# Expert slots of 32, 64 and 64 + 32 tokens in plain float32 in a two-block kernel, and a state-space product whose two column halves alternate

## Chip, cores and metric

One core of a Trainium2 chip. The metric is device time in microseconds of the whole program; lower is better.

## The reference

Two transformer-like blocks over 512 tokens of width 1024, batch 1, float32. The first block mixes tokens (an in-projection, two state-space scans with heads of 64, a Fourier branch, an output projection) and then runs a mixture of 32 experts; the second is attention beside a gated recurrence, with a dense feed-forward. The part at issue is mostly the mixture: each token goes to its four best experts, and an expert's work on the rows it got is

```python
gu = xe @ w_gate_up[e] + b_gate_up[e]                       # 1024 -> 2048
gate = jnp.minimum(gu[:, :D_FF], SWIGLU_LIMIT)
up = jnp.clip(gu[:, D_FF:], -SWIGLU_LIMIT, SWIGLU_LIMIT)
act = (up + 1.0) * gate * jax.nn.sigmoid(SWIGLU_ALPHA * gate)
return act @ w_down[e] + b_down[e]                          # 1024 -> 1024
```

weighted by the softmax of the four logits and added to the token. Each expert has 12 MB of float32 weights, 384 MB for all 32, and 512 x 4 = 2048 rows are shared out among them, 64 on average. The reference's own routing of its inputs gives experts 0 and 1 25 and 23 rows; the other thirty, sorted, get 16 to 30 (six of them), 34 to 63 (eight), 66 to 95 (twelve), 109, 128, 130 and 155.

## The kernel before, in words

**The mixture (`moe`, from L1169).** The experts are put into 32 slots: slots 0 and 1 are experts 0 and 1, the others are sorted by load on the chip (`router`, `slot` and `perm`). A slot has a fixed room: slots 0 to 15 (`HALF`) one block of 64 rows, 16 to 29 one of 128, 30 and 31 (`DOUBLE`) one of 128 and one of 64. What doesn't fit goes through a loop at the end (`For_i`), one block of 128 rows a pass. `ORDER` is the order in which the slots are worked on, one slot a turn.

A turn is `up` of its own slot and then `down` of the slot before. `up` walks through eight raw tiles of `w_gate_up` of 1 MB each (L61), `down` through four of `w_down` (L1348). All loads go out on SyncE's queue, in the order of their use, into a ring of 13 tiles (`W.rings`): a load is issued when the tile 13 loads earlier has been read for the last time. So the loads run at most 13 tiles, about one turn, ahead.

- A block of 128 rows works on weights split into a high part (ScalarE, L86) and a low part (VectorE, L87) in a format that TensorE takes at one row of the moving operand after the other; each product is three matmuls (`mm3`, L99 to L101): 12 matmuls of 512 columns per MB.
- A block of 64 rows takes the raw weights in plain float32 (`half_mm`, L1262): the rows are stationary, 64 columns of the array wide, and the two halves of the output columns go to the two halves of the array. The profile shows a float32 matmul as two instructions, so there are 8 per MB.

In a turn with two blocks, `up` and `down` go through both blocks for each tile of weights. Around this lie the gather of the rows (GpSimd, L1227), their transposes on TensorE (L1245, L1240 for halves), the bias matmuls (L1254), the activation (`swiglu`, L1267 to L1270), the scaling of the result (ScalarE L1331, GpSimd L1336) and the scatter that adds to the token's row (L1337). Two steps hooked into `up` make the tables of later blocks (`table`, L1075 to L1081; `slots`) and transpose the previous slot's activations; one hooked into `down` transposes the next slot's rows. For slot 0 the rows aren't gathered but picked out by matmuls in `router` (L975).

**The state-space part (`mixer`).** For each of 16 pairs of heads, `py` collects 16 products of float32 (two heads j, two directions d, four blocks b of 128 tokens; L669), each two instructions on 64 columns of the array: head 0 writes partitions 0 to 63, head 1 partitions 64 to 127. The loops run j, d, b from outside in. The masks `m` come by DMA (L619) in the order j, d.

Two places in the first half load `w_mod` and multiply it by one vector with 32 stationary columns, four such matmuls into the four quarters of the array (L266, L515).

Of the kernel before, what the change touches and what calls it, by code (L numbers as in the profile page):

```python
# [8 lines left out]
F32 = mybir.dt.float32  # L9
# [95 lines left out]
TILE_WAITS = ('moeio', 'moeio3', 'ps_g', 'ps_mt', 'ps_d', 'outr', 'outp', 'mx', 'biasp', 'rows', 'b2io', 'b2t', 'b2r', 'res2', 'moeT', 'wraw3', 'wraw4')  # L105


class Kernel:
# [91 lines left out]
    def mixer(self):  # L200
# [391 lines left out]
        for p in range(16):  # L592
# [22 lines left out]
            for j in range(2):  # L615
                for d in range(2):
# [269 lines left out]
    def router(self, mx, keep, xT, ahead, st, stp):  # L886
# [59 lines left out]
        def choose(b, x1, rs, fill=lambda: None):  # L946
# [23 lines left out]
            self.chosen = nc.vector.tensor_scalar(pick[:, b, :], iota[:, 0:64], r[:, 0:1], None, op0=ALU.is_equal).ins  # L970
# [18 lines left out]
        pick = xT[:, 0:256].rearrange("p (b l) -> p b l", l=64)  # L989
# [17 lines left out]
        xT4 = xT[:, 512:].rearrange("p (k t) -> p k t", k=4)  # L1007
        nc.scalar.copy(xT4[:, 0:2, :], pts[0][:, 0:2, :])
        nc.vector.tensor_copy(xT4[:, 2:4, :], pts[0][:, 2:4, :])
        ahead()  # L1010

        with self.behind((self.chosen,)):
            p0 = psl.tile([P, 1, 3], F32, tag='ptab', name='ptab0')
            self.table(rot, p0[:, 0, :], rm[:, :, 1:2], V[:, :, 1, 0:3], True, True)
            first = self.slots(keep, p0, 1, 'f', (0,))[0]
# [53 lines left out]
    def table(self, pool, out, place, v, first, half=False):  # L1069
# [3 lines left out]
        v4 = lambda x: x.rearrange("p b (h l) -> p b h l", h=2)  # L1073
        if half:
            nc.vector.tensor_tensor(v4(pe), self.rc[:, 0, None, None, 0:64].to_broadcast([P, NT, 2, 64]),  # L1075
                                    place[:, :, :, None].to_broadcast([P, NT, 2, 64]), op=ALU.is_equal)
# [16 lines left out]
    def overflow(self, tp, psl, selb, ubf, obf, keep):  # L1093
# [3 lines left out]
        nc, cf = self.nc, self.rc  # L1097
# [10 lines left out]
        val = tp.tile([P, 2, 16], BF16, name='val')  # L1108
        for i, c in enumerate((16, 40)):
            nc.vector.tensor_scalar(val[:, i, :], cf[:, 2, 24:40], pos, cf[:, 2, c:c + 1], op0=ALU.is_equal, op1=ALU.mult)  # L1110
        nc.tensor.matmul(pc[:, 8:40], obf, val.rearrange("p i q -> p (i q)"), start=True, stop=True,
                         skip_group_check=True)
        nc.tensor.matmul(pc[:, 40:41], obf, fl, start=True, stop=True, skip_group_check=True)
        self.ext = ext = keep.tile([P, 33], F32, name='ext')
        nc.vector.tensor_copy(ext, pc[:, 8:41])

        no = tp.tile([P, 16], F32, name='noblk')
        nc.vector.tensor_scalar(no, ext[:, 16:32], 0.0, 4096.0, op0=ALU.is_equal, op1=ALU.mult)
        nc.vector.tensor_add(ext[:, 16:32], ext[:, 16:32], no)
        self.exti = keep.tile([P, 33], I32, name='exti')  # L1120
# [23 lines left out]
    def slots(self, pool, tab, n, sfx, halves=()):  # L1144


        nc = self.nc
        t = pool.tile([P, n, tab.shape[2]], F32, name='slott' + sfx)
# [6 lines left out]
        for j in halves:  # L1155
            nc.vector.tensor_scalar(f[:, 0, j:j + 1], f[:, 0, j:j + 1], 2.0, self.rc[:, 2, 41:42], op0=ALU.mult, op1=ALU.add)
        nc.vector.tensor_copy(i, f[:, 0, :])
        if tab.shape[2] > 3:
# [5 lines left out]
    HALF = range(0, 16)  # L1164
    DOUBLE = (30, 31)
    ORDER = (0, 1, 16, 17, 2, 3, 18, 19, 4, 20, 5, 21, 6, 30, 7, 8, 22, 9, 23, 10, 24, 11, 31, 12, 13, 25, 26, 14, 27, 28,
             29, 15)

    def moe(self, mx):  # L1169
# [39 lines left out]
        halfrows = lambda t: t.rearrange("s (h c) -> (s h) c", h=2)  # L1209
# [7 lines left out]
        io3 = self.pool('moeio3', 4, None, st)  # L1217
# [7 lines left out]
        def gather(i, tok, half=False):  # L1225
            x = xgs[i % 2]
            nc.gpsimd.indirect_dma_start(out=x[:, :D // 2] if half else x, out_offset=None,  # L1227
                                         in_=halfrows(self.h2_d) if half else self.h2_d,
                                         in_offset=bass.IndirectOffsetOnAxis(ap=tok, axis=0),
                                         bounds_check=(2 * S if half else S) - 1, oob_is_err=False)  # L1230
            return x

        def transposed(half, src, scale):
# [3 lines left out]
            if half:  # L1237
                h = src[:, 512:].rearrange("p (k t) -> p k t", k=4)
                for k in range(4):
                    nc.tensor.transpose(pt[:, k, :], src[:, k * P:(k + 1) * P], self.ident)  # L1240
                nc.scalar.activation(h, pt[:, 0:4, :], AF.Copy, scale=scale)  # L1241
                return half, h
            h = Ts[next(turns) % 2]
            for k in range(KD):
                nc.tensor.transpose(pt[:, k, :], src[:, k * P:(k + 1) * P], self.ident)  # L1245
            split_scaled(nc, h, pt, scale)
            return half, h

        def bias(half, outs, selT, c):

            w = 64 if half else P
            for i, o in enumerate(outs):
                for q in range(P // w):
                    nc.tensor.matmul(o[w * q:w * q + w], selT.to_broadcast([96, w]),  # L1254
                                     bh[:, c + 512 * (i * (P // w) + q):][:, :512], start=True, stop=False,
                                     skip_group_check=half)
# [15 lines left out]
        def up(xTs, rows, selT, step=None):  # L1272

            acts, pgs = [], []
            for half, _ in xTs:
                acts.append((half, io3.tile([P, D], F32, tag='row', name='act')))
                if not half:
                    pgs.append([bank2(ps_g, 'pg', 'pg') for _ in range(2)])
                    for i in range(2):
                        bias(half, (pgs[-1][i][:, 0, :], pgs[-1][i][:, 1, :]), selT, D * i)  # L1280
                else:
                    pgs.append(bank2(ps_d, 'pd', 'pgh') if len(xTs) == 2 else bank2(ps_g, 'pg', 'pgh'))
                    bias(half, (pgs[-1][:, 0, :], pgs[-1][:, 1, :]), selT, 0)
            for k, raw in enumerate(rows):
                for (half, x), pg in zip(xTs, pgs):
                    for h in range(2):
                        if half:
# [707 lines left out]
```

## Time and profile before

| what | value |
|---|---|
| median of 3 runs (2915.26 to 2928.36) | 2924.7 us |
| the profiled execution's own time | 2918.13 us |
| its span, first to last instruction | 2916.3 us |
| mean granted TensorE clock | 0.984 of full speed |
| bytes moved by DMA | 644.40 MB |

PE is TensorE's matmuls, PEld its loads of the stationary operand, DVE VectorE, ACT ScalarE, POOL GpSimd, SP SyncE, whose instructions here only issue loads. In the rows, `out<-in` names the tiles, 128\*64 means 128 rows and 64 columns of the array, and x is a count. A matmul's duration holds its way through the array, so a string of matmuls is priced by the distance from one start to the next.

### The profile page before, as it was taken

To read this page: it belongs to the slowest core of one execution; us is meant where nothing else is said; L and a number is where in the kernel's file an instruction comes from. 1 tells how busy PE (TensorE), PEld (TensorE's weight loads), DVE (VectorE), ACT (ScalarE), POOL (GpSimd) and SP (SyncE) were. 2 spreads that over 40 slices of the span, in tenths; PEclk is the share of its full clock that TensorE was granted. 3 is DMA by queue.
4 is the path that set the end of the run, shared out by engine and by line. 5 is a ranking of instruction groups with operands and counts; after the bars stand their busy time and mean duration, and the time that the engine had idled before them with its cause. 6 is when DMAs were issued, how large, how long until landed. Compare 5 with 4: busy or idle time off the path is not lost. (4 is left out here: it accounts for less than half of the span.)

```text
span 2916.3 us, 37264 instructions
## 1 busy us (share of the span) xinstructions
PE 2772.1 (95%) x14084; PEld 2033.2 (70%) x14084; DVE 1773.7 (61%) x2557; ACT 1321.1 (45%) x1899; POOL 403.5 (14%) x388
## 2 busy tenths in 40 slices
PE   5999999999999999999999999999599999999999
PEld 3888878788887455555455554657288888788887
DVE  4637878787677565766445552768477777733322
ACT  4534545454444244544334442556356666632221
POOL 1211121212202111111111112120300000100000
PEclk9999999999999899999999999999799999999999
DMA  8243374744566899999699979998532132533321
GB/s 229 80 137 96 113 220 134 228 126 138 179 188 246 343 387 401 359 391 400 258 402 408 389 293 386 399 382 342 147 101 83 55 87 73 188 97 91 101 94 65
DMA packets 294839, 644.40 MB, mean 221 GB/s; under 512 B 18706, under 2 KB 190370, under 8 KB 258848
## 3 DMA queue, kind: packets, MB, share of 16 engines
q1 hardware_dynamic: 267552, 569.77, 53.3%
q0 software_dynamic: 25120, 67.93, 8.6%
q10 hardware_dynamic: 1984, 4.28, 0.4%
q8 instruction: 112, 1.84, 0.3%
q14 instruction: 71, 0.58, 0.1%
HBM read 617.54 MB, written 33.64 MB: 223 GB/s over the span
## 5 line engine op out<-in xcount | busy, mean ns | idle before, releaser
L87 DVE TENSOR_TENSOR wlo<-wraw,whi 128x1024 fp32r<-128x1024 f32 (+1 forms) x635 | 787.8, 1264 | 462.1 <-ACT whi L86 451.5
L86 ACT CAST whi<-wraw 128x1024 fp32r<-128x1024 f32 (+1 forms) x635 | 652.5, 1043 | 605.5 <-PE pf L100 153.2
L1262 PE MATMUL pgh<-wraw,xg 128*64 128x512 f32 x1152 | 279.7, 605 | 0.7 <-ACT xg L1241 0.7
L99 PE MATMUL px<-hThi,whi 128*128 128x512 f32 x576 | 229.9, 400 | 0.0
L101 PE MATMUL px<-hThi,wlo 128*128 128x512 f32 x576 | 225.9, 392 | 2.1 <-DVE wlo L87 2.1
L100 PE MATMUL px<-hTlo,whi 128*128 128x512 f32 x576 | 226.4, 393 | 0.0
L1262 PEld LDWEIGHTS pgh<-wraw,xg 128*64 128x64 f32 x1152 | 81.8, 138 | 154.0 <-issue 147.6
L1336 POOL TENSOR_TENSOR y<-y,g2b 64x512 f32<-64x512 f32 (+1 forms) x50 | 86.1, 1723 | 522.2 <-ACT y L1331 497.4
L100 PE MATMUL pg<-wlo,T0h 128*128 128x512 f32 x352 | 144.2, 410 | 5.5 <-DVE wlo L87 5.4
L100 PE MATMUL pf<-hnlo,whi 128*128 128x512 f32 (+1 forms) x384 | 142.4, 372 | 0.0
L101 PE MATMUL pf<-hnhi,wlo 128*128 128x512 f32 (+1 forms) x384 | 142.4, 372 | 0.0
L99 PE MATMUL pf<-hnhi,whi 128*128 128x512 f32 (+1 forms) x384 | 141.6, 372 | 0.0
L101 PE MATMUL pg<-whi,T0l 128*128 128x512 f32 x352 | 140.4, 399 | 0.0
L99 PE MATMUL pg<-whi,T0h 128*128 128x512 f32 x352 | 132.4, 405 | 3.4 <-ACT whi L86 3.4
L484 DVE SCALAR_TENSOR_TENSOR cacc<-cr,vecs,cacc 128x770 f32<-128x770 f32 (+1 forms) x128 | 121.7, 961 | 19.8 <-ACT cacc L482 18.7
L101 PEld LDWEIGHTS px<-hThi,wlo 128*128 128x128 f32 x576 | 108.3, 188 | 27.6 <-DVE wlo L87 2.9
L1262 PE MATMUL pd<-wraw,act 128*64 128x512 f32 x512 | 122.7, 599 | 0.0
L100 PEld LDWEIGHTS px<-hTlo,whi 128*128 128x128 f32 x576 | 109.0, 189 | 16.0 <-issue 1.7
L99 PEld LDWEIGHTS px<-hThi,whi 128*128 128x128 f32 x576 | 109.0, 189 | 15.7 <-issue 1.7
L1267 DVE TENSOR_SCALAR g<-pgh 128x512 f32<-128x512 f32 x18 | 12.4, 691 | 170.4 <-PE pgh L1262 170.3
L1268 ACT ACTIVATE g<-g 128x512 f32<-128x512 f32 (+1 forms) x34 | 28.2, 831 | 178.9 <-DVE g L1267 178.9
L623 ACT ACTIVATE m<-m,acs_tok 128x128 f32<-128x128 f32 x256 | 81.6, 390 | 58.3 <-DMA m<-acs_scr 56.6
(614 smaller groups left out, 6102.3 us busy)
## 6 DMA issues: line engine op xcount, KB each, us to landing
wraw<-in_w_gate_up SPq DMA_DIRECT2D x256, 1024.0 KB, 9.7
wraw<-in_w_down SPq DMA_DIRECT2D x128, 1024.0 KB, 9.9
wraw<-in_w_in SPq DMA_DIRECT2D x81, 512.0 KB, 6.6
wraw<-in_w_mod SPq DMA_DIRECT2D x23, 1024.0 KB, 9.1
wraw<-in_w_ffn_in SPq DMA_DIRECT2D x44, 512.0 KB, 5.2
wraw<-in_w_in SPq DMA_DIRECT2D x18, 1024.0 KB, 5.4
m<-acs_scr POOLq DMA_DIRECT2D x64, 256.0 KB, 5.3
wraw<-in_w_ffn_out SPq DMA_DIRECT2D x10, 1024.0 KB, 5.0
```

The lines of the kernel that those rows point to most:

```text
L86: a = (copy or nc.scalar.copy)(dst[0], src)
L87: return a.ins, (eng or nc.vector).tensor_sub(dst[1], src, dst[0].bitcast(F32)).ins
L99: nc.tensor.matmul(out, a[0], b[0], start=first, stop=False)
L100: nc.tensor.matmul(out, a[0], b[1], start=False, stop=False)
L101: return nc.tensor.matmul(out, a[1], b[0], start=False, stop=last).ins
L484: nc.vector.scalar_tensor_tensor(acc, t[:, j:j + n], cw[:, j, ch:ch + 1], acc, op0=ALU.mult, op1=ALU.add)
L623: nc.scalar.activation(m[:, b, :], m[:, b, :], AF.Relu, bias=acs_tok[:, b, row:row + 1], scale=-1.0)
L1262: nc.tensor.matmul(out[64 * h:64 * h + 64], a, w, start=False, stop=last, skip_group_check=True)
L1267: nc.vector.tensor_scalar_min(g, gate, 7.0)
L1268: nc.scalar.activation(g, g, AF.Silu, scale=1.702)
L1336: nc.gpsimd.tensor_mul(y[q], y[q], g2b[q, c])
```

## The change

- Rooms: slots 0 to 7 one block of 32 rows, 8 to 15 one of 64, 16 to 27 one of 64 and one of 32, 28 and 29 one of 128, 30 and 31 one of 128 and one of 64 (`WIDTHS`). 46 blocks in place of 34. `ORDER` is new.
- A block of 32 rows works like one of 64, in plain float32 on raw weights, with four quarters of the array in place of two halves: per MB of `w_gate_up` 8 instructions of 512 columns, per 128 rows of `w_down` 8 of 256.
- Token rows are gathered and scattered in pieces of 1 KB for blocks of 32 (2 KB for 64, 4 KB for 128).
- The tiles for activations and results come in two sizes from two pools: 3 of 1024 columns, 4 of 512.
- The pick for slot 0 in `router` has 32 columns; the overflow list has 24 places in place of 16, and its limits follow the rooms.
- `py`: the loops run d, b, j, and the masks are made in the order d, j.

```diff
-            for j in range(2):
-                for d in range(2):
+            for d in range(2):
+                for j in range(2):
                     row = 32 * d + h0 + j
                     m = pr4.tile([P, NT, P], F32, tag='m', name='m')
...
-            for j in range(2):
-                for d in range(2):
-                    for b in range(NT):
-                        nc.tensor.matmul(py[j * HD:(j + 1) * HD, b, :], xd[d][:, b, j, :], ms[2 * j + d][:, b, :],
+            for d in range(2):
+                for b in range(NT):
+                    for j in range(2):
+                        nc.tensor.matmul(py[j * HD:(j + 1) * HD, b, :], xd[d][:, b, j, :], ms[2 * d + j][:, b, :],
...
-                nc.tensor.matmul(pts[0][:, k % 4, 64 * (k // 4):64 * (k // 4) + 64], h2s[b][0][:, k * P:(k + 1) * P],
+                i, o = k % n0, k // n0 * w0
+                nc.tensor.matmul(pts[0][:, i, o:o + w0], h2s[b][0][:, k * P:(k + 1) * P],
...
-    HALF = range(0, 16)
-    DOUBLE = (30, 31)
-    ORDER = (0, 1, 16, 17, 2, 3, 18, 19, 4, 20, 5, 21, 6, 30, 7, 8, 22, 9, 23, 10, 24, 11, 31, 12, 13, 25, 26, 14, 27, 28,
-             29, 15)
+    WIDTHS = ((8, (32,)), (16, (64,)), (28, (64, 32)), (30, (128,)), (32, (128, 64)))
+    ORDER = (0, 1, 16, 2, 8, 17, 9, 30, 18, 10, 19, 20, 3, 11, 31, 4, 5, 28, 21, 22, 23, 6, 24, 25, 12, 13, 26,
+             27, 14, 29, 15, 7)
...
-        io3 = self.pool('moeio3', 4, None, st)
+        io3 = self.pool('moeio3', 3, None, st)
+        io4 = self.pool('moeio4', 4, None, st)
...
+        def columns(w, x):
+            n = P // w
+            v = x.rearrange("p (g q c) -> p g q c", q=n, c=D // n)
+            return [v[:, :, q, :] for q in range(n)]
...
-        def half_mm(out, xT, k, ws, last):
-            a = xT[:, k % 4, 64 * (k // 4):64 * (k // 4) + 64]
-            for h, w in enumerate(ws):
-                nc.tensor.matmul(out[64 * h:64 * h + 64], a, w, start=False, stop=last, skip_group_check=True)
+        def part_mm(w, out, xT, k, ws, last):
+            n = KD * w // P
+            a = xT[:, k % n, k // n * w:k // n * w + w]
+            for i, o in enumerate(out):
+                for q, wq in enumerate(columns(w, ws)):
+                    m = wq.shape[1] // len(out)
+                    nc.tensor.matmul(o[w * q:w * q + w], a, wq[:, m * i:m * i + m, :], start=False, stop=last,
+                                     skip_group_check=True)
...
+            for k, raw in enumerate(chunks):
+                for (w, x), pg in zip(xTs, pgs):
+                    if w < P:
+                        part_mm(w, pg, x, k, flat(raw), k == KD - 1)
+                        continue
...
+            for c, raw in enumerate(chunks):
+                for (w, a), pd in zip(aTs, pds):
                     for j in range(2):
                         k = 2 * c + j
+                        if w < P:
+                            part_mm(w, (pd[:, 0, :8 * w],), a, k, flat(raw[:, 2 * j:2 * j + 2, :]), k == KD - 1)
...
-                for q, c in qs:
+                for i in range(P // w):
+                    q, c = slice(w * i, w * i + w), slice(n * i, n * i + n)
...
                         nc.gpsimd.tensor_mul(y[q], y[q], g2b[q, c])
```

## Rows read from the trace of the kernel before

**Rows 1.** The page: busy time of each engine, and PE's share in 40 slices.

```profile
PE 2772.1 (95%) x14084; PEld 2033.2 (70%) x14084; DVE 1773.7 (61%) x2557; ACT 1321.1 (45%) x1899; POOL 403.5 (14%) x388
PE   5999999999999999999999999999599999999999
DMA  8243374744566899999699979998532132533321
```

**Rows 2.** Busy time by stretch, state-space and mixture: us, engines, clock, DMA share, GB/s.

```profile
255.00:780.00 525.00, 523.83 (x3214) 444.27 (x3212) 403.36 (x705) 259.36 (x531) 107.72 (x178) 1.00 0.51 153
...
952.00:2077.00 1125.00, 1075.61 (x4802) 610.38 (x4798) 643.79 (x713) 498.32 (x519) 187.00 (x115) 0.99 0.93 362
```

**Rows 3.** PE's matmuls of py by stretch: all, then within one pair of heads.

```profile
255.00:780.00 525.00, 53.67 (x512) 49.33 (x512) 11.96 (x16) 1.00 0.51 153
...
259.00:260.20 1.20, 1.20 (x11) 1.20 (x12) 1.00 0.00 0
260.36:260.74 0.38, 0.38 (x10) 0.38 (x9) 1.00 0.00 0
```

**Rows 4.** What PE waited for between 255 and 780 us: total, times, longest.

```profile
PE pm L515 <- DMA wraw<-in_w_mod: 0.3, 1, 0.3
```

**Rows 5.** Groups of instructions in the mixture: count, busy us, mean ns, idle before.

```profile
L87 DVE TENSOR_TENSOR wlo<-wraw,whi 128x1024 fp32r<-128x1024 f32 x384 | 473.6, 1270 | 135.9 <-ACT whi L86 133.8 <-DMA wraw<-in_w_gate_up 1.5
L86 ACT CAST whi<-wraw 128x1024 fp32r<-128x1024 f32 x384 | 393.5, 1048 | 159.1 <-PE pg L101 103.1 <-PE pd L101 35.2 <-DMA wraw<-in_w_gate_up 7.3
```

**Rows 6.** PE in order of time, slot 30: start, us, instruction; then another 64-row block.

```profile
1408.98 1.94 PE L1262 MATMUL pgh<-wraw,xg 128*64 128x512 f32 x8
...
1411.19 0.39 PE L101 MATMUL pg<-whi,T0l 128*128 128x512 f32 x1
...
1413.52 0.40 PE L99 MATMUL pg<-whi,T0h 128*128 128x512 f32 x1
1413.85 1.94 PE L1262 MATMUL pgh<-wraw,xg 128*64 128x512 f32 x8
...
1538.95 13.95 PE L1262 MATMUL pgh<-wraw,xg 128*64 128x512 f32 x64
```

**Rows 7.** PE in order of time: matmuls of 32 columns, in mid-kernel and at its start.

```profile
553.14 1.07 PE L515 MATMUL pm<-wraw,sc 128*32 128x512 f32 x8 [0.33 <-DMA wraw<-in_w_mod]
554.14 0.50 PE L100 MATMUL px<-hTlo,whi 128*128 128x512 f32 x1
...
10.21 1.94 PE L266 MATMUL pm<-wraw,sc 128*32 128x512 f32 x8 [1.95 <-DMA wraw<-in_w_mod]
```

**Rows 8.** DMA from 1000 to 2050 us: GB/s in 40 slices, queues, microseconds to landing.

```profile
GB/s 410 411 362 364 406 413 371 362 356 392 380 407 405 385 360 192 257 412 383 414 411 410 404 380 408 383 400 210 240 410 416 399 402 381 396 398 349 355 346 333
...
q1 hardware_dynamic: 67359, 374.95, 89.3%
q0 software_dynamic: 7779, 14.79, 5.6%
...
wraw<-in_w_gate_up SPq DMA_DIRECT2D x230, 1024.0 KB, 9.7
```

**Rows 9.** What the load queue, then PE, waited for in the mixture: total, times, longest.

```profile
SPq L61 <- DVE wlo L87: 240.9, 100, 6.5
SPq L61 <- PE pgh L1262: 211.1, 100, 13.1
SPq L1348 <- DVE wlo L87: 147.2, 52, 6.1
...
PE pg L100 <- DVE wlo L87: 8.7, 11, 1.2
```

**Rows 10.** PE's wait after slot 0, and GpSimd's groups in the mixture.

```profile
978.33 1.12 PE L1240 MATMUL pt<-ident,xg 128*128 128x128 f32 x4 [1.37 <-DVE slott L1149]
...
L1337 POOL DMA_INDIRECT x_scr<-y,sloti x32 | 62.6, 1956 | 16.2 <-DMA x_scr<-y,sloti 8.0 <-POOL y L1336 4.5 <-issue 3.5
L1336 POOL TENSOR_TENSOR y<-y,g2b 64x512 f32<-64x512 f32 x34 | 47.3, 1392 | 223.5 <-ACT y L1331 198.6 <-DMA xg<-h_scr,sloti 15.1 <-DMA x_scr<-y,sloti 7.2
L1227 POOL DMA_INDIRECT xg<-h_scr,sloti x32 | 37.3, 1164 | 392.1 <-PE pt L1245 175.4 <-DVE wlo L87 75.9 <-PE pt L1240 47.9
```

More of the change, by code (lines that the diff above doesn't have):

```diff
@@ L1142, in extra, with slots @@
         return r[:, 0, :, None], v
-    def slots(self, pool, tab, n, sfx, halves=()):
-        nc = self.nc
-        t = pool.tile([P, n, tab.shape[2]], F32, name='slott' + sfx)
+    def slots(self, pool, tab, sfx, widths, tmp=None):
+        nc, n = self.nc, len(widths)
+        t = (tmp or pool).tile([P, n, tab.shape[2]], F32, name='slott' + ('' if tmp else sfx))
         nc.vector.tensor_copy(t, tab)
@@ L1161, in slots, with widths @@
         return i, f[:, 1, :]
-    HALF = range(0, 16)
-    DOUBLE = (30, 31)
-    ORDER = (0, 1, 16, 17, 2, 3, 18, 19, 4, 20, 5, 21, 6, 30, 7, 8, 22, 9, 23, 10, 24, 11, 31, 12, 13, 25, 26, 14, 27, 28,
-             29, 15)
+    WIDTHS = ((8, (32,)), (16, (64,)), (28, (64, 32)), (30, (128,)), (32, (128, 64)))
+    ORDER = (0, 1, 16, 2, 8, 17, 9, 30, 18, 10, 19, 20, 3, 11, 31, 4, 5, 28, 21, 22, 23, 6, 24, 25, 12, 13, 26,
+             27, 14, 29, 15, 7)
+    NX = 24
+    @classmethod
+    def widths(cls, slot):
+        return next(ws for n, ws in cls.WIDTHS if slot < n)
     def moe(self, mx):
@@ L1231, in gather, with transposed @@
             return x
-        def transposed(half, src, scale):
+        def transposed(w, src, scale):
             pt = bank2(ps_t, 'pt', 'pt').rearrange("p h (k t) -> p (h k) t", t=P)
[L1237 to L1244, printed above, removed]
-                nc.tensor.transpose(pt[:, k, :], src[:, k * P:(k + 1) * P], self.ident)
-            split_scaled(nc, h, pt, scale)
-            return half, h
@@ new lines, in transposed @@
+            for k in range(n):
+                nc.tensor.transpose(pt[:, k, :], src[:, k * P:(k + 1) * P], self.ident)
+            if w < P:
+                h = src[:, src.shape[1] // 2:][:, :n * P].rearrange("p (k t) -> p k t", k=n)
+                nc.scalar.activation(h, pt[:, 0:n, :], AF.Copy, scale=scale)
+            else:
+                h = Ts[next(turns) % 2]
+                split_scaled(nc, h, pt, scale)
+            return w, h
+        def columns(w, x):
+            n = P // w
+            v = x.rearrange("p (g q c) -> p g q c", q=n, c=D // n)
+            return [v[:, :, q, :] for q in range(n)]
@@ new lines, in bias @@
+        def bias(w, out, selT, c, n):
+            b = bh[:, c:c + D * n]
+            if w == P:
+                for i, o in enumerate(out):
+                    nc.tensor.matmul(o, selT.to_broadcast([96, P]), b[:, 512 * i:512 * i + 512], start=True, stop=False)
+                return
+            for q, bq in enumerate(columns(w, b)):
+                for i, o in enumerate(out):
+                    g = n // len(out)
+                    nc.tensor.matmul(o[w * q:w * q + w], selT.to_broadcast([96, w]), bq[:, g * i:g * i + g, :],
+                                     start=True, stop=False, skip_group_check=True)
@@ L1359, in moe @@
         for s_ in self.ORDER:
-            blocks += [(s_, 0, s_ in self.HALF)] + ([(s_, P, True)] if s_ in self.DOUBLE else [])
+            ws = self.widths(s_)
+            blocks += [(s_, sum(ws[:i]), w) for i, w in enumerate(ws)]
         at = lambda e: [i for i, b in enumerate(blocks) if b[0] == e]
@@ L1369, in step @@
                 if j < n:
-                    e, o, half = blocks[i0 + j]
+                    e, o, w = blocks[i0 + j]
                     src = self.rm[:, :, e:e + 1]
@@ L1374, in step @@
                         nc.vector.tensor_scalar_add(src, self.rm[:, :, e:e + 1], -float(o))
-                    self.table(io, ptab[:, j, :], src, self.V[:, :, e, :], j == 0, half)
+                    self.table(io, ptab[:, j, :], src, self.V[:, :, e, :], j == 0, w)
                 if j == n - 1:
-                    t = self.slots(keep, ptab, n, str(i0), [i for i in range(n) if blocks[i0 + i][2]])
+                    t = self.slots(keep, ptab, str(i0), [b[2] for b in blocks[i0:i0 + n]], io)
                     for i in range(n):
@@ L1389, in moe @@
             nx = at(self.ORDER[turn + 1]) if turn < NE - 1 else []
+            assert not (nx and len(xTs) == 2 and xTs[0][0] < P and blocks[nx[0]][2] == P)
             if e < 2:
```

160 lines of the change are left out of this document (76 added, 84 removed).

## The prediction

> **What bounds the kernel now.** I read the page first: PE, the matmul engine, is busy 95% of the span and in nearly every slice [rows 1]. A busy share doesn't say what a stage could gain, so next the stretches: the change touches two, the state-space part from 255 to 780 us and the mixture from 952 to 2077 us [rows 2].
>
> In the state-space part PE is busy 523.8 of 525 us, with DVE at 77%, ACT at 49% and DMA at 51% [rows 2]; the list of waits has a single entry for PE, of 0.3 us [rows 4]. PE alone is the bound: what is taken from it there should come off the end nearly whole.
>
> The mixture looks the same (PE 1075.6 of 1125 us), but DMA has a share of 0.93 [rows 2]. Two things could be the limit, and the waits tell which. The load queue waits for casts and matmuls to give a tile back, 241, 211 and 147 us in its three longest entries, and PE's waits are a few us each and for casts [rows 9]. So loads follow PE, and PE is the bound, with DMA close behind: take much from PE and the loads become the bound.
>
> **The py loop.** 512 matmuls take 53.67 us, 0.105 us each [rows 3]: in one half of the array at a time. Only where head 0 hands over to head 1 are both halves at work: 10 matmuls show in 0.38 us there, 11 in 1.2 us elsewhere [rows 3]. A row of the mixture says the same: a 64-column matmul of 512 columns comes every 0.213 us (64 in 13.95, less a last 0.5 of draining [rows 6]), while eight with 32 columns take 0.87 us less than eight with 64 (1.07 against 1.94 [rows 6, 7]): as many as fit beside each other run together. With j innermost the two halves alternate, so half the 53.67 goes: **-27 us**. At least -13, if halves only partly overlap or DVE, at 77%, holds up a pair; at most -28. Making the masks in the order d, j moves two DMAs of four past each other on GpSimd's queue; they are ready long before py, and cost nothing (POOL is busy 108 of 525 us [rows 2]).
>
> **What a block costs on PE.** 128 rows: 12 matmuls per MB, one every 0.233 us (1411.19 to 1413.52 is ten of them [rows 6]), so 2.80 us per MB and 33.6 us for 12 MB. 64 rows: 96 at 0.213, 20.5 us. 32 rows: the row with four quarters has eight in 1.00 us from its start to the next instruction's, switching included [rows 7]; two rounds of 0.427 are 0.85. So 8 MB of gate and up take 6.9 us, and down with half as many columns 3.4: 10.3 us.
>
> A block of 64 and one of 32 take turns within each MB, so the array changes from halves to quarters and back 12 times per expert. No row shows that change. The nearest is the one between full width and halves in slot 30: 1408.98 to 1413.85 is 4.87 us for eight halves (1.71) and twelve full matmuls (2.80) [rows 6], so 0.36 us for there and back. Halves and quarters are closer kinds, so bounds are 0 and 0.36; I take the middle, 0.18. Such an expert then costs 10.3 + 20.5 + 2.2 = 33.0 us, against 33.6 for the full block it replaces: the twelve save PE almost nothing. The eight experts that go from 64 to 32 save 10.2 us each, 82 us in all.
>
> The Trainium skill, "TensorEngine Tiling (Array Packing)", section "Key Properties", says that a change of tiling mode drains the engine. That speaks against the change; the row agrees for full width and halves, no run here shows halves against quarters, and by the page alone the price would be the 0.36 and the mixture 16 us longer than I forecast.
>
> **What the rest of a turn costs.** Matmuls of the 18 blocks of 64 and 16 of 128, and 2 x 12 changes, make 916 us. The other 209 of the 1125 are biases, transposes, tables and short waits. Split by what each turn issues, that is 7.45 us for a turn with 128 rows (twice the transposes, and cast waits [rows 9]), 5.4 for 64, and I put 4.3 for 32, 7.2 for 64 + 32. A turn on PE: 14.6 us (32), 25.9 (64), 40.2 (64 + 32), 41.1 (128), 68.8 (128 + 64).
>
> **What a turn's loads cost.** From 1000 to 2050 us the hardware queue moved 374.95 MB in 89.3% of 1050 us, 2.62 us per MB tile, and the software queue (gathers, scatters) took 5.6%, 59 us for some 31 blocks of each [rows 8]. 12 x 2.62 + 1.9 = 33.3 us a turn. After the change gathers and scatters carry the same bytes in smaller pieces: between the same 59 us and, if each block cost alike, 46/34 of it; I take 33.5 us a turn.
>
> **The ledger.** Go through `ORDER`, adding PE's turn less the loads'. Below zero PE waits, so the lag stays at zero; above 33 us (13 tiles ahead, a turn) the ring is full and the loads idle. The stretch is 32 turns of loads, less 18 us loaded before 952, plus idle loads, plus the last lag. Before: 1048 + 50 + 26 = 1123 us, against 1125 measured; the loads idle mostly after 30 and 31, where the GB/s fall to 192 and 210 [rows 8]. After: 32 x 33.5 - 18 = 1054, plus 23 of idle loads (after 30, 20 and 31), plus no lag: 1077 us, **-46 us**. With the change of mode at 0 it is -52, at 0.36 -30.
>
> **What hides the rest.** 288 of 384 casts go: 366 us of DVE, 302 of ACT [rows 5]; both stood beside PE, so only the short waits end. Tiles of 64-row blocks now go back after their last matmul, not after a cast, some two tiles later than a full block's: that shortens the lead, within the bounds. POOL gets 12 more gathers (1.16 us) and scatters (1.96), and the scaling of a 32-row block is four pieces, at most 1.39 us each [rows 10]: at most +130 us on 187 busy of 1125; the next rows are needed a turn later, so that is hidden, and if POOL stuck, the transposes of the next rows would stand in PE's queue. Tables for 12 more blocks are in the turn costs. The tiles in two sizes cost nothing while a scatter lands within a turn (a load lands in 9.7 us [rows 8]). Slot 0's matmuls get 10 us shorter, but PE then stood waiting for DVE's slot numbers (978.33 [rows 10]), so nothing comes of it. In turns of 32 PE idles between loads and may slow down: eight matmuls took 1.94 us at the start of the kernel, fed by loads alone [rows 7]; that is still under 2.62 per load.
>
> **Sum.** -27 - 46 = -73 us. Against the profiled execution's own 2918.1 that is 2845; the median shown is 6.6 higher, so I say 2850.
>
> **Rivals.**
> *Loads at their best* (0.20): changes of mode cost nothing and the ring never empties. The loads' own time, 0.93 x 1125 = 1046 us, is the floor; -79 and -28 make 2811. For it: slices of 410 to 416 GB/s [rows 8]. Against: slots 30 and 31 still starve the loads.
>
> *PE stays the bound* (0.13): 0.36 per change, and the later return of tiles costs some 10 us more. -20 and -20 make 2878.
>
> *The loads are already the bound* (0.07): then the mixture doesn't move and only py's 27 us come: 2891, 2898 for the median. For it: 0.93 of DMA. Against: the load queue waits for tiles [rows 9], and the mean of 362 GB/s [rows 2] lies well under 416. The Trainium skill, "DMA: Bandwidth & Descriptors", section "Specifications", has about 358 GB/s as HBM's limit per core; by that the loads would be the bound today. The slices above 400 GB/s contradict it.
>
> *Quarters run two at a time* (0.06), the slower side: a 32-row block then costs 20.5 us, like one of 64, and the ledger gives 1229 us, +104; less 27 that is 2995. It turns slower when a 32-row block passes 15 us (ledger 1140), 0.16 us per matmul. Against: eight in 1.07 us [rows 7].
>
> *Overflow* (0.04): rooms too small, so that the loop runs. Each pass is a turn with nothing beside it, about 33 + 41 us; two make it slower, 2918 - 73 + 148 = 2993. Against: the loads of the experts as the reference routes them fit every room, up to 30 of 32, 63 of 64, 95 of 96, 128 of 128.
>
> **How the numbers follow.** The forecast gets 0.50. Range: from the floor less some of the spread of the runs, 2803, to PE staying the bound plus the median's offset and some spread, 2893; beyond lie the last two rivals and part of the third. A measurement here tells 0.5%, 14.6 us, from no change. Faster: forecast, floor, PE bound and most of the third, 0.89; same: the rest of the third and near misses, 0.04; slower: 0.07 of the last two.
>
> **What would show it.** After: py's row at about 27 us busy for 512; 96 casts; the mixture near 1077 us, DMA share 0.97 or more, PE waiting for DMA in turns of 32; the eight-matmul rows with 32 columns near 0.85 us; a distance from 64 to 32 and back that gives the price of the change. I am wrong if the loads' share falls under 0.93, if rows of 32 columns take twice as long, or if PE in the state-space part begins to wait.

## The result, and the profile after

The changed kernel takes **2839.1 us** (median of 4 runs, 2838.5 to 2840.5) against 2924.4 us for the kernel before: a ratio of 0.9713, 95% interval 0.969 to 0.9736. The forecast was 2850 us. The profiled execution took 2838.98 us, with a span of 2837.2 us, 79.1 less than the 2916.3 of before.

The page of the changed kernel, as in [rows 1]: PE's busy time and share, then PE and DMA in 40 slices.

```profile
PE 2674.4 (94%) x15382; PEld 1772.2 (62%) x15382; DVE 1409.0 (50%) x2373; ACT 1021.8 (36%) x1659; POOL 472.8 (17%) x486
PE   5999999999998989999999989988499999999999
DMA  8243465744565999999999999999612212533321
```

PE now has slices of 8 within the mixture, and DMA is at 9 in all of its slices; before, it fell to 6 and to 7. The stretches that answer to [rows 2], cut at the first and last matmul: the state-space part from the first to the last py, the mixture, and the gap from the mixture's last matmul to the second block's first product. First the kernel before, then the changed one (columns: length; busy time of PE, PEld, DVE, ACT, POOL; granted clock, DMA share, GB/s).

```profile
259.00:776.70 517.70, 517.37 (x3180) 439.23 (x3179) 397.40 (x691) 257.89 (x529) 107.72 (x178) 1.00 0.51 153
951.60:2077.00 1125.40, 1076.01 (x4802) 610.58 (x4801) 644.19 (x713) 498.32 (x519) 187.00 (x115) 0.99 0.93 362
2077.00:2110.10 33.10, 1.04 (x9) 0.94 (x9) 16.06 (x18) 9.49 (x18) 19.95 (x10) 0.54 0.52 141
```

```profile
259.30:761.00 501.70, 500.34 (x3180) 418.33 (x3179) 395.87 (x691) 256.08 (x529) 106.58 (x177) 1.00 0.52 157
937.90:1992.40 1054.50, 991.21 (x6100) 366.62 (x6099) 281.29 (x526) 200.10 (x279) 254.96 (x212) 0.98 0.98 386
1992.50:2029.90 37.40, 1.03 (x8) 0.92 (x8) 16.45 (x20) 9.51 (x18) 21.52 (x11) 0.50 0.50 143
```

So: -16.0 us in the state-space part, of which 13.7 are left where the mixture begins (951.6 to 937.9), **-70.9 in the mixture**, +4.3 in the gap, and about +1 behind it.

The mixture's waits of the changed kernel, as in [rows 9]: PE's two longest entries, then the four longest of the load queue (us in total, times, longest).

```profile
PE pgh L1288 <- DMA wraw<-in_w_gate_up: 21.0, 17, 4.3
PE pd L1288 <- DMA wraw<-in_w_down: 10.5, 12, 1.6
...
SPq L61 <- PE pgh L1288: 191.4, 91, 13.0
SPq L1378 <- DMA wraw<-in_w_gate_up: 135.2, 66, 8.4
SPq L1378 <- PE pd L1288: 122.0, 41, 24.7
SPq L61 <- DMA wraw<-in_w_down: 110.9, 57, 3.3
```

Before, no wait of PE for a load was on the list, and wlo led the queue's. Now PE waits 31.5 us for loads, the casts are gone from the queue's first four entries, and two of the four are loads behind earlier loads. With a DMA share of 0.98 the loads mostly set the pace; e4 and e9 below show how nearly PE is level with them.

### The profile page after: what moved, and what is told of

The parts are those of the page before. It is cut to its first block, busy times and chain, and to the rows that moved or that the text cites. A ratio compares the mean times of both kernels' runs of the same rounds, so it can differ in the third digit from the quotient of the medians.

```text
span 2837.2 us, 39216 instructions
## 1 busy us (share of the span) xinstructions
PE 2674.4 (94%) x15382; PEld 1772.2 (62%) x15382; DVE 1409.0 (50%) x2373; ACT 1021.8 (36%) x1659; POOL 472.8 (17%) x486
## 5 line engine op out<-in xcount | busy, mean ns | idle before, releaser
L87 DVE TENSOR_TENSOR wlo<-wraw,whi 128x1024 fp32r<-128x1024 f32 (+1 forms) x347 | 434.6, 1263 | 372.7 <-ACT whi L86 364.3
L86 ACT CAST whi<-wraw 128x1024 fp32r<-128x1024 f32 (+1 forms) x347 | 358.2, 1041 | 503.8 <-PE pf L100 153.2
L1288 PE MATMUL pgh<-wraw,xg 128*64 128x512 f32 (+1 forms) x2688 | 507.3, 609 | 21.6 <-DMA wraw<-in_w_gate_up 21.0
L1288 PEld LDWEIGHTS pgh<-wraw,xg 128*64 128x64 f32 (+1 forms) x2688 | 122.9, 124 | 321.6 <-issue 271.6
L1366 POOL TENSOR_TENSOR low<-low,g2b 32x256 f32<-32x256 f32 (+1 forms) x120 | 124.3, 1036 | 329.3 <-ACT low L1360 215.1
L1288 PE MATMUL pd<-wraw,row 128*64 128x512 f32 x640 | 154.8, 607 | 3.0 <-DMA wraw<-in_w_down 3.0
L99 PEld LDWEIGHTS px<-hThi,whi 128*128 128x128 f32 x576 | 109.7, 190 | 16.4 <-issue 1.7
L1241 POOL DMA_INDIRECT xg<-h_scr,sloti x44 | 47.8, 1087 | 388.8 <-PE pt L1252 285.8
L99 PE MATMUL px<-h2hi,whi 128*128 128x512 f32 x256 | 104.0, 406 | 0.0
L100 PE MATMUL px<-h2lo,whi 128*128 128x512 f32 x256 | 102.8, 402 | 0.0
L101 PE MATMUL px<-h2hi,wlo 128*128 128x512 f32 x256 | 100.7, 393 | 0.0
```

The source lines that it names most:

```text
L86: a = (copy or nc.scalar.copy)(dst[0], src)
L87: return a.ins, (eng or nc.vector).tensor_sub(dst[1], src, dst[0].bitcast(F32)).ins
L99: nc.tensor.matmul(out, a[0], b[0], start=first, stop=False)
L100: nc.tensor.matmul(out, a[0], b[1], start=False, stop=False)
L101: return nc.tensor.matmul(out, a[1], b[0], start=False, stop=last).ins
L1241: nc.gpsimd.indirect_dma_start(out=x[:, :D * w // P], out_offset=None, in_=rows(self.h2_d, w), in_offset=bass.IndirectOffsetOnAxis(ap=tok, ...
```

## The experiments

Ratios are to the kernel before on the same chip, whose median there was 2918.3 to 2920.1 us. "Mixture" is the stretch from its first to its last matmul in the profile.

**The py loops alone, in half of the pairs, and everything but py.** e1 is the kernel before with the diff's two hunks in `mixer`; e10 takes them for the last 8 of 16 pairs; e12 is the changed kernel with them undone (the hunk of the loops is shown, that of the masks goes with it).

> The kernel before with nothing but the two py loops and the mask order of the change. Theory from the changed kernel's trace: a string of 32 py matmuls goes from 3.06 to 1.69 us from first to last start, 16 pairs of heads, 22 us of PE time; PE loses some 4 us of that again to the other order of the matmuls that load w_mod's product (L515), so the state-space part ends some 15 us earlier and the whole comes out at about 2909 us, ratio 0.995 (0.994 to 0.9955), with the mixture unmoved. The prediction's term: -27 us, 2898 us, ratio 0.991. Rival: the part's saving is given back before the mixture's first matmul, ratio over 0.998.

> The changed kernel with the py loops and the mask order of the kernel before, all else as changed. Theory: py is worth 14 to 15 us where the state-space part ends, and in the changed kernel nothing of it is lost again, because a mixture at the pace of the loads doesn't feel how often the clock falls; so 13 to 16 us slower than the changed kernel: a ratio to the kernel before of 0.976 to 0.978, 2850 to 2857 us. Rival: py is worth 4 to 6 us here too, as when it was changed alone: a ratio of 0.973 to 0.9745, 2843 to 2847 us. The prediction's term, 27 us, would give 2866 us.

```diff
-            for d in range(2):
-                for b in range(NT):
-                    for j in range(2):
-                        nc.tensor.matmul(py[j * HD:(j + 1) * HD, b, :], xd[d][:, b, j, :], ms[2 * d + j][:, b, :],
+            for j in range(2):
+                for d in range(2):
+                    for b in range(NT):
+                        nc.tensor.matmul(py[j * HD:(j + 1) * HD, b, :], xd[d][:, b, j, :], ms[2 * j + d][:, b, :],
```

e1: 2914.5 us, 0.9981 (0.9972 to 0.999), some 5 us. e12: 2857.3 us, 0.9787 (0.9767 to 0.9806), which is 0.006 to 0.0074 more than the changed kernel's two ratios (0.9713, and 0.9727 in e5 below), 17 to 22 us, each uncertain by 7 to 9 by the intervals; its profiled span is 17.1 us longer than the changed kernel's and 12.1 longer than e5's, and its mixture begins 15.5 us later than the changed kernel's. So the same edit is worth 5 us in one kernel and some 17 in the other, and the intervals leave no overlap. For e12 the theory came out, at its upper end or past it. For e1 only the rival's number did (over 0.998): its mechanism, a saving given back before the mixture's first matmul, didn't, and neither did the theory's unmoved mixture. Where e1's gain went shows in the window of its mixture:

```profile
937.70:2072.90 1135.20, 1081.91 (x4802) 618.31 (x4801) 649.24 (x713) 499.76 (x519) 189.10 (x115) 0.98 0.93 359
```

It begins 13.9 us earlier than in the kernel before and lasts 9.8 us longer, with the same instructions, PE busy for 5.9 us more, and a clock of 0.98 in place of 0.99. Summed over stretches of 5 us, what the granted clock lacked of full speed comes to 26.1 us in e1's mixture and to 16.0 in that of the kernel before: the 10 us between them match the 9.8 that were lost. The timelines show one place of this kind, the same step of the program in both kernels. First e1, then the kernel before (start, duration, in brackets the idle time and what ended it):

```profile
1355.38 0.34 PE L1081 MATMUL ptab<-V,pe 128*128 128x6 bf16 x8 [0.70 <-ACT xg L1241]
...
1359.23 0.80 PE L100 MATMUL pd<-wlo,T1h 128*128 128x512 f32 x1 [0.56 <-DVE wlo L87]
1359.82 0.63 PE L101 MATMUL pd<-whi,T1l 128*128 128x512 f32 x1
...
1364.94 0.62 PE L101 MATMUL pd<-whi,T1l 128*128 128x512 f32 x1
1365.37 0.42 PE L99 MATMUL pd<-whi,T1h 128*128 128x512 f32 x1
```

```profile
1365.48 0.34 PE L1081 MATMUL ptab<-V,pe 128*128 128x6 bf16 x8 [0.69 <-ACT xg L1241]
...
1369.54 0.80 PE L100 MATMUL pd<-wlo,T1h 128*128 128x512 f32 x1 [0.53 <-DVE wlo L87]
1370.13 0.63 PE L101 MATMUL pd<-whi,T1l 128*128 128x512 f32 x1
...
1372.69 0.48 PE L101 MATMUL pd<-whi,T1l 128*128 128x512 f32 x1
1373.00 0.40 PE L99 MATMUL pd<-whi,T1h 128*128 128x512 f32 x1
```

After a few short pauses (2.5 us in all in e1, 2.9 in the kernel before) the matmuls take 0.63 us and follow each other at 0.43, where 0.23 is usual: the granted clock is 0.50, the level of 1.2 GHz. In e1 that goes on to 1365.4, 6.1 us from the end of the wait for wlo; in the kernel before only to 1373.0, 3.5 us. Over all runs, time goes with clock: 17 runs of the kernel before reach from 2913.7 us at 0.986 to 2926.4 at 0.980, while e1's 12 runs all lie at 0.979 to 0.981 and 2913.4 to 2915.9, some 12 us under the runs of before at 0.980.

> The kernel before with the changed py loop and mask order in the last 8 of the 16 pairs of heads alone. Up to the mixture it should be some 7 us ahead of the kernel before. Theory: what py alone lost again in the mixture is lost to how PE's short pauses there fall, after which the granted clock is half for some us, and that depends on nothing but when the mixture starts: so the time goes with the clock as in the kernel before (some 2 us for each 0.001), 5 to 9 us below what the kernel before has at the same clock (2913.7 at 0.986, 2926.4 at 0.980), whatever clock it gets. Rival: the py change itself makes the mixture longer in proportion; then half of both, a ratio of 0.999 and a clock midway, 0.982.

e10: 2911.4 us, 0.9974 (0.9965 to 0.9983), clocks 0.982 to 0.985. At 0.983 its runs took 2909.9 to 2913.5 us, the kernel before 2919.0 to 2919.9: some 7 us less at the same clock, as the theory has it. The rival fell: it had a ratio of 0.999 and a clock of 0.982, while the interval ends at 0.9983 and the mean clock of e10's runs is 0.983, the same as that of the kernel before on its chip. Half of the edit so gained 7 us, more than the whole of it in e1. That e1's gain is lost to the clock is shown; why the clock falls more often in every run of e1 stays open. In the changed kernel the clock no longer decides: its mixture, e5's and e12's lack 25.4, 33.2 and 32.0 us of full speed and take 1054.5, 1056.1 and 1053.9 us.

**Order, eight, twelve: one at a time.** All keep the changed `py` and the changed `ORDER`; only `WIDTHS` differs: e8 has the rooms of before, e3 the twelve of 64 + 32 alone, e2 the eight of 32 alone. So e8 has, beside `py` and the order, the rest of the change's code too, such as the two pools of tiles.

```diff
-    WIDTHS = ((8, (32,)), (16, (64,)), (28, (64, 32)), (30, (128,)), (32, (128, 64)))
+    WIDTHS = ((16, (64,)), (30, (128,)), (32, (128, 64)))               # e8
+    WIDTHS = ((16, (64,)), (28, (64, 32)), (30, (128,)), (32, (128, 64)))   # e3
+    WIDTHS = ((8, (32,)), (16, (64,)), (30, (128,)), (32, (128, 64)))   # e2
```

> The changed kernel with its py loops and its order of slots, but with the rooms of the kernel before: slots 0 to 15 one block of 64 rows, 16 to 29 one of 128, 30 and 31 one of 128 and one of 64. What the order alone does. The prediction's ledger: the mixture at 1127 to 1131 us, 5 to 7 us more than the kernel before; with the py loops 2908 to 2925 us. Rival: the new order is itself worth most of the 26 us by which the mixture was shorter with the twelve of 64 + 32 and without the eight of 32; then 2885 to 2897 us, and the twelve are worth nothing in that kernel either.

> The changed kernel, but slots 0 to 7 have one block of 64 rows again: what the twelve of 64 + 32 and the order bring without the eight of 32. The prediction's ledger with the change of width at 0.18 to 0.31 us puts the mixture at 1123 to 1139 us against 1125 for the kernel before: all of the mixture's gain is gone, 2900 to 2920 us. Rival: the eight experts' PE time was hidden under the loads anyway and the gain came from the casts; then the mixture stays under 1085 us, 2870 us or less. In PE work alone it should be 82 us more than the changed kernel's (8 x 10.2).

> The changed kernel, but slots 16 to 27 have one block of 128 rows again (34 blocks): what the eight experts of 32 rows and the new order bring without the twelve of 64 + 32. The prediction's ledger: twelve experts cost PE 41.1 us a turn instead of 40.2, the mixture 1080 against 1077 us, so within 10 us of the changed kernel: 2842 to 2850 us. Rival: what the twelve bring isn't PE time but the end of the casts, on which loads and PE waited; then the mixture is 20 us or more longer than the changed kernel's 1054 us, 2860 us or more, with the load queue's waits for wlo back above 100 us and DMA's share near 0.95.

The windows of the three mixtures, e8, e3, e2:

```profile
937.60:2053.80 1116.20, 1062.91 (x4802) 611.07 (x4801) 649.26 (x712) 499.25 (x519) 192.41 (x115) 0.99 0.94 366
```

```profile
938.80:2038.60 1099.80, 1062.99 (x5858) 396.17 (x5857) 291.63 (x526) 205.14 (x279) 251.53 (x197) 0.99 0.95 370
```

```profile
939.40:1989.30 1049.90, 982.37 (x5044) 585.57 (x5043) 641.13 (x712) 492.37 (x519) 200.60 (x129) 0.97 0.98 388
```

| kernel | time, us | ratio (interval) | mixture, us | PE's work, us |
|---|---|---|---|---|
| before | 2919.7 | 1 | 1125.4 | 1062 |
| e1: py | 2914.5 | 0.9981 (0.9972 to 0.999) | 1135.2 | 1060 |
| e8: py, order (old rooms) | 2893.7 | 0.9908 (0.9893 to 0.9923) | 1116.2 | 1050 |
| e3: py, order, twelve | 2889.9 | 0.9897 (0.988 to 0.9914) | 1099.8 | 1051 |
| e2: py, order, eight | 2835.8 | 0.9716 (0.97 to 0.9732) | 1049.9 | 960 |
| the change | 2839.1 | 0.9713 (0.969 to 0.9736) | 1054.5 | 971 |

PE's work is its busy time in the mixture times the granted clock, summed over stretches of 5 us; it is uncertain by some 2. Four things follow.

- The **order**, with whatever the rest of the new code does at the old rooms, is worth about 20 us of e8 against e1, where the ledger had +5 to +7: its rival's end, and outside the 2908 to 2925 us expected. No run has the order by itself. Half of it is e1's clock: e8's mixture lacks 15.8 us of full speed where e1's lacks 26.1. 9 us of the mixture remain against the kernel before, which has e8's clock.
- The **eight** blocks of 32 are the change: PE's work falls by 90 us (e8 to e2; my 82), the time by 56 to 58, because the loads catch it: DMA from 0.94 to 0.98.
- The **twelve** save PE nothing, 1050 in e8 and 1051 in e3. The time moved by 4 us there, within the two intervals, and by nothing beside the eight. They do end the casts (DVE 649 to 292 us), and e3's mixture is 16.4 us shorter than e8's; but the gap behind it is 12 us longer (43.2 against 31.2 us, by PE's wait in the rows below; the last scatter starts 20.9 us behind the last matmul, in e8 8.5), so that hardly anything reaches the end. e3 fits neither its expectation (2900 us or more, off by what e8 gained) nor its rival (2870 or less).
- Beside the eight, the casts covered nothing: e2 is as fast as the whole change. Its rival, casts as the bound, fell, though the queue's waits for wlo came back (183.2 and 144.0 us).

PE's first matmul behind the mixture, e8 and e3:

```profile
2071.11 1.03 PE L1566 MATMUL pm<-ident,mn 16*128 16x16 f32 x8 [17.31 <-DVE mn L1563]
```

```profile
2067.90 1.03 PE L1566 MATMUL pm<-ident,mn 16*128 16x16 f32 x8 [29.28 <-DMA x<-x_scr]
```

**Is it PE or the loads?** e4 takes work from PE, e9 from the loads.

```diff
-                for (w, x), pg in zip(xTs, pgs):
+                for (w, x), pg in turned(zip(xTs, pgs), xTs, k):
...
+        turned = lambda ps, ws, k: list(ps)[::-1 if len(ws) == 2 and ws[0][0] < P and k % 2 else 1]
```

> The changed kernel, but in an expert of 64 + 32 rows the two blocks take turns as 64, 32, 32, 64 from tile to tile, so the width changes half as often: 6 there-and-backs an expert fewer, 72 in all. At the 0.31 us that the changed kernel's trace shows for there and back this is 22 us of PE time. Theory, the loads are the bound now: PE's busy time falls by about 20 us and its waits for loads grow by nearly as much, the time by 0 to 6 us, 2833 to 2839 us. Rival, PE is still the bound in the mixture: the time falls by 15 to 22 us, 2817 to 2824 us. Rival, the 0.31 us are not a price of the change of width: PE's busy time doesn't move.

```diff
             for i in range(4):
-                t = W.raw()
-                nc.sync.dma_start(out=t.rearrange("p (t n c) -> p t n c", t=2, n=2), in_=v[:, i])
+                if i < 3:
+                    t = W.raw()
+                    nc.sync.dma_start(out=t.rearrange("p (t n c) -> p t n c", t=2, n=2), in_=v[:, i])
```

> The changed kernel without every fourth tile of w_down: the last quarter of an expert's down product multiplies the third tile again, so 32 of the mixture's 384 MB aren't loaded and as much is computed as before. Theory, the loads set the pace of the mixture: at 2.6 us per MB they take 83 us less; PE, whose own work is some 1023 us of the mixture's 1054 (31 us are waits for loads) and gets shorter as its clock falls less often, becomes the bound, so the time falls by 30 to 60 us, to 2780 to 2810 us, and PE's waits for loads all but go. Rival, PE sets the pace: the time falls by less than 10 us, 2829 us or more.

The windows of the mixtures of e4 and e9, then e9's only two waits of PE for loads there:

```profile
940.20:1983.60 1043.40, 980.09 (x6100) 381.10 (x6099) 275.04 (x526) 199.48 (x279) 250.84 (x212) 0.96 0.99 390
```

```profile
937.80:1971.10 1033.30, 992.86 (x6100) 370.73 (x6099) 282.05 (x526) 198.94 (x279) 256.73 (x213) 0.98 0.93 362
```

```profile
PE pgh L1288 <- DMA wraw<-in_w_gate_up: 6.3, 7, 1.5
PE pd L1288 <- DMA wraw<-in_w_down: 2.2, 2, 1.5
```

e4: 2833.2 us, 0.9708 (0.969 to 0.9726), 1 to 6 us less than the change. PE's work is 951 in place of 971, close to the 22 us expected, so the change of width has its price on PE. The time hardly follows. I had expected PE's waits for loads to grow, and they didn't (26.1 us; 31.5 in the changed kernel, 26.2 in e5); the clock falls to 0.96 instead. So the loads cover most of this price, but not all: in the profiles the mixture is 11 us shorter than the changed kernel's. e9: 2815.7 us, 0.9645 (0.9628 to 0.9662), 20 to 24 us less than the change by the ratios, under the 30 to 60 expected and over the rival's 10. With 32 MB fewer PE hardly waits for loads and sets the pace again, at 1033 us. **PE stands only some 21 us behind the loads** (1054.5 - 1033.3). Less work on either side shortens the mixture by a part of it: the change has brought the two nearly level.

**The gap behind the mixture.** GpSimd's queue in the changed kernel, from the last scaling to the last scatter:

```profile
1982.80 2.61 POOL L1366 TENSOR_TENSOR low<-low,g2b 64x512 f32<-64x512 f32 x2 [15.32 <-ACT low L1360]
1985.69 1.58 POOL L1367 DMA_INDIRECT x_scr<-low,sloti  x1 [0.28 <-POOL low L1366]
1993.52 1.59 POOL L1367 DMA_INDIRECT x_scr<-row,sloti  x1 [6.25 <-DMA x_scr<-low,sloti]
2002.06 1.57 POOL L1367 DMA_INDIRECT x_scr<-low,sloti  x1 [6.95 <-DMA x_scr<-row,sloti]
2007.73 1.55 POOL L1367 DMA_INDIRECT x_scr<-low,sloti  x1 [4.10 <-DMA x_scr<-low,sloti]
```

From the second on, every scatter waits for the one before to land, and the four are those of slots 14, 29, 15 and 7. Slot 14's result is scaled by 1936, but the program's order has its scatter behind the scaling of slot 15, which waits for ScalarE until 1982.8. In the kernel before two scatters are left after the last matmul, here three, the last 15.3 us after it.

> The changed kernel once more, unaltered, as the measure for the kernels beside it on the same chip. Expected: 2832 to 2841 us and a ratio of 0.971 to the kernel before; its time should hardly move with the mean granted clock, if the loads set the pace of the mixture, while the kernel before moves some 2 us with each 0.001 of it (17 runs from 0.986 at 2913.7 to 0.980 at 2926.4 us).

> The changed kernel, but the results of the last three slots but one (14, 29, 15) are scaled on VectorE straight out of PSUM, as the last slot's already are, in place of ScalarE and GpSimd. GpSimd's queue then holds no scaling of a later slot ahead of an earlier slot's scatter. Theory: four scatters, one after the other at 7 to 8 us each, stand behind the last matmul because GpSimd's queue has each of them behind a later slot's scaling; with that gone only the last one is left, it starts some 12 us earlier, and the time falls by 8 to 13 us against the changed kernel on the same chip. Rival: the chain of scatters is held up by their landing alone; then nothing moves (within 3 us).

```diff
-                down(aT, *prev[1:], down_step)
+                down(aT, *prev[1:], down_step, tail=turn >= NE - 3)
```

The same stretch of GpSimd's queue in e6, whose mixture ends at 1999.5:

```profile
1966.73 1.58 POOL L1367 DMA_INDIRECT x_scr<-row,sloti  x1 [10.63 <-DVE row L1364]
1990.30 1.57 POOL L1367 DMA_INDIRECT x_scr<-low,sloti  x1 [21.99 <-DVE low L1364]
2001.88 1.55 POOL L1367 DMA_INDIRECT x_scr<-low,sloti  x1 [10.00 <-DMA wraw<-in_w_in]
```

One scatter is left, 2.4 us after the last matmul; the gap is 26.1 us, against 38.7 in e5. e5 took 2841.6 us (up to 2841 were expected), 0.9727 (0.9714 to 0.974), e6 2834.5, 0.9703 (0.969 to 0.9716). That is 7 us less, a little under the 8 to 13 expected; in the profiled runs the gap gave 12.6 and the mixture took 3.5 back.

**Together.** e7 adds to e6 the turns of e4, and keeps the matmuls of `w_mod` behind po's:

```diff
-                        mod_rest(g - 1)
+                        with self.behind([po_last]):
+                            mod_rest(g - 1)
```

> The changed kernel with three alterations: the last three slots but one scaled on VectorE, the width changing half as often in experts of 64 + 32, and the matmuls of w_mod (L515) kept behind po's, so that quarters aren't mixed in between full-width matmuls. Theory: -10 from the tail, -4 from L515, 0 to -6 from the flips, as the loads set the pace of the mixture: 14 to 20 us less than the changed kernel on the same chip. Rival: what the state-space part gives is given back in the mixture, as when py was changed alone: 8 to 13 us less.

> The changed kernel with the last slots' scaling on VectorE, the matmuls of w_mod behind po's, and slots 16 to 27 with one block of 128 rows: 34 blocks and no change of width within those experts. Theory: the twelve of 64 + 32 are worth nothing, as PE's work is the same with and without them and the loads set the pace; 2815 to 2824 us, the same as the three alterations with the twelve (2820.5 us, ratio 0.9657). Rival: with the tail and the w_mod matmuls mended the casts come back as the bound: over 2830 us.

e7: **2820.5 us, 0.9657** (0.9644 to 0.967), 21 us less than the change on the same chip (e5), where 14 to 20 were expected. Its state-space part, from first to last py, is 498.6 us against 501.7, its mixture 1047.7, its gap 26.7. The rival, that the state-space part's gain would be lost again in the mixture, fell. e11, which has no expert of 64 + 32 and no turns, is as fast: 2821.5 us, 0.9666 (0.9646 to 0.9686). Both beat both kernels.

## Why the prediction was right, point by point

The mechanism was right in the main, the sizes less so. Against -73 stand -79.1 us in the profiled runs, but that is in part luck: py brought some 11 us less than its term, the mixture 25 more.

**What bounds the kernel.** Right in both stages: the state-space part gave up what PE was spared there, and the mixture passed from PE to the loads (share 0.98; 0.97 or more was the sign), with PE close behind.

**The py loop, -27 us: mis-sized.** It was 16 to 17. One pair's py in the kernel before, then in the changed one, each with the instruction behind it:

```profile
291.91 3.33 PE L669 MATMUL py<-m,xd 128*64 128x128 f32 x32
295.17 0.94 PE L677 MATMUL po<-C,Hn 128*128 128x128 f32 x6
```

```profile
426.25 1.97 PE L669 MATMUL py<-m,xd 128*64 128x128 f32 x32
428.14 1.05 PE L677 MATMUL po<-C,Hn 128*128 128x128 f32 x7
```

A pair goes from 3.26 to 1.89 us to the next start: 16 x 1.37 = 22. Both halves do run together, but 1.89 is more than half of 3.26. From first to last start a string went from 3.06 to 1.69 us: two strings side by side run not quite at the pace of one, which costs 2.5 us in the 16 pairs. The last matmul's way through the array, 0.27 us, isn't halved, and I took half of a busy time that holds it 16 times: 2 us more. The rest went to an instruction order that I had not thought of: the matmuls of `w_mod` (L515), which came behind po in one string, are now mixed in between po's. Their two rows, before and after:

```profile
404.96 2.78 PE L515 MATMUL pm<-wraw,sc 128*32 128x512 f32 x24
```

```profile
397.37 1.04 PE L515 MATMUL pm<-wraw,sc 128*32 128x512 f32 x2
398.34 0.49 PE L677 MATMUL po<-C,Hn 128*128 128x128 f32 x2
398.76 1.04 PE L515 MATMUL pm<-wraw,sc 128*32 128x512 f32 x2
399.74 1.16 PE L677 MATMUL po<-C,Hn 128*128 128x128 f32 x8
400.82 2.77 PE L515 MATMUL pm<-wraw,sc 128*32 128x512 f32 x20
```

24 in 2.71 us became 0.97 + 0.98 + 2.70, here and at a second place (533.4 us): 3.9 us. e7, which keeps them behind po's, has 3.1 us of the part's length back. New waits of PE for xs and whi (1.0 and 0.4 us) are part of the last 2; what the remainder is, isn't shown. The bound of -13 held.

**What a block costs.** 32 rows and the four quarters were right (64 matmuls of 256 columns at the end of e2's mixture took 3.64 us; the sum has 3.4, without the last one's way), and so was "the twelve save PE almost nothing" (e3 against e8). The **change of width** was under-priced. Within an expert of 64 + 32, in the changed kernel:

```profile
1354.95 1.94 PE L1288 MATMUL pd<-wraw,row 128*64 128x512 f32 x8
1356.82 1.07 PE L1288 MATMUL pd<-wraw,low 128*32 128x256 f32 x16
1357.82 1.94 PE L1288 MATMUL pd<-wraw,row 128*64 128x512 f32 x8
```

2.87 us from one string of halves to the next, less 1.71 for the halves and 0.85 for the quarters (16 of half the columns), is 0.31 us there and back, where I took 0.18 between 0 and 0.36. The Trainium skill's rule ("TensorEngine Tiling (Array Packing)", "Key Properties") that a change of mode drains the engine fits halves against quarters too; the price is this run's, and e4 bears it out. It did not cost the time what the ledger said, as e4 shows as well.

**The rest of a turn: over-priced, by about as much.** PE's turns summed to 1026 us in my ledger; measured are 1054.5 less 31.5 of waits for loads, 1023, with 0.31 in place of 0.18 (144 changes, +19). The rest was smaller by some 20 us. Part of that are PE's waits for casts: 20.4 us in the mixture before (its three longest entries), 7.7 in the changed one. That two errors cancelled is luck.

**The loads and the ledger, -46: mis-sized; it was -71.** The queues' shares in the mixture, from the kernel before (952.4 to 2077.0) and the changed one (938.3 to 1992.4):

```profile
q1 hardware_dynamic: 71049, 390.82, 87.1%
q0 software_dynamic: 8240, 15.84, 5.7%
```

```profile
q1 hardware_dynamic: 70412, 390.07, 91.9%
q0 software_dynamic: 9410, 15.76, 6.2%
```

Loads, gathers and scatters took 93.1% of 1124.6 us before, 1047 us with the small queues, and 98.4% of 1054.1 = 1037 us after. I had 32 x 33.5 - 18 = 1054: 6 us for smaller pieces, which cost 1 (0.057 x 1124.6 = 64 us against 65), and loads at an unchanged 2.62 us per MB that now come in at 2.60; why they do isn't shown. Idle are 17 us in place of 23. So the mixture ended close to my rival "loads at their best" (1046 plus nothing), and the total between that rival and the forecast; its condition, changes of width at no cost, was wrong, the ring that hardly empties right. What I missed besides is the share of e8: the ledger gave the order a few us of loss, e8 shows a gain of 9 in the mixture.

**What hides the rest.** The casts cost nothing beside the eight, as e2 shows; slot 0's shorter matmuls and the tables no run sets apart. Not hidden was GpSimd: I let a scatter that lands within a turn pass, but behind the last turn there is no other to hide it: +4.3 us in the gap. e6 shows that 12.6 were there to be had, this loss among them.

**The other rivals.** "PE stays the bound" fell, though its price per change (0.36) was nearer than mine: the mixture gained 71 us, not 20. "Loads already the bound" fell by the same 71 us. On the Trainium skill's 358 GB/s ("DMA: Bandwidth & Descriptors", "Specifications") the mixture couldn't have been shorter than before; its mean is now 386 GB/s. Quarters two at a time, and overflow, didn't occur.

## What to carry to other kernels

When two resources are close (here PE at 1125 us and the loads at 1047 us in the mixture before), sum up both for every turn, and expect the gain to shrink where the second one begins: of 90 us taken from PE 56 to 58 came off the time, of 20 more only 1 to 6. Test each part of a change by itself, in the kernel where it will live: py was worth 5 us in a kernel bound by PE and some 17 in one bound mostly by loads, and the twelve double blocks were worth nothing at the end of the program. Look also at the stage behind the one that got shorter: there the twelve lost their 16 us, and there a reordered queue had put scatters behind the last matmul. When two strings are to run side by side, halve only the stretch from first to last start and not the busy time.

## What the runs showed of the hardware that I had not expected

Much the same pauses of PE (2.9 and 2.5 us in all, at the same step of the program) were followed by 3.5 us at a granted clock of half in the kernel before and by 6.1 in e1, in which the mixture began 14 us earlier. In the runs of the kernel before, a mean granted clock lower by 0.001 went with some 2 us of the whole. The Trainium skill ("TensorE: Matmul & The Clock Gate", "What's actually happening") says that the chip's watch on activity runs freely and isn't restarted with a kernel, and that the point at which the clock changes varies for this reason. The spread of the kernel before (0.980 to 0.986) agrees; that all 12 runs of e1 lie within 0.979 to 0.981 is not explained by it. Of the changed kernel's last scatters, which add to rows in memory, each let the next one start only 5.7 to 8.5 us after its own start.
